# A hybrid decoder layer on one core: the down product written in a fixed order for three engines, its last block product bank by bank over five steps, and the row factors of the final norm in fewer operations

## The chip, the core and the metric

The kernel runs on one core of a Trainium2 chip. The metric is the device time of one execution in microseconds, the median over runs. One further execution was taken with the hardware profiler; its records are the trace that is read here.

## The reference

```python
def reference(x, mem, norm_mix, w_in, ..., w_up, conv_w, conv_b, w_down, norm_final):
    h = x
    for l in range(DEPTH):
        ...
        h = h + conv_ffn(rms_norm(h, norm_ffn[l]), w_up[l], conv_w[l], conv_b[l], w_down[l])
    return rms_norm(h, norm_final)

def conv_ffn(h, w_up, conv_w, conv_b, w_down):
    u = h @ w_up
    ...
    gate, val = jnp.split(u, 2, axis=-1)
    return (jax.nn.silu(gate) * val) @ w_down
```

What is left out is the token mixing, the cross attention and a causal convolution of width 3. All in fp32: 1024 rows of 1024, one layer, and an inner width of 2816. The change touches the last product, `(silu(gate) * val) @ w_down` (1024 x 2816 by 2816 x 1024), the residual sum with `h` and the final `rms_norm`.

## The kernel before

A fp32 product is made of three fp32r matmuls. `split` (L105) turns a source tile of 128 x 512 into an *operand*: ScalarE casts it to its high part (L109), VectorE subtracts that from the source to get the low part (L110), and TensorE adds up high x high, high x low and low x high. An operand pair (left and right) is used in one *step*: four PSUM banks (128 rows of the output by 512 columns each) times three matmuls, 12 in all (L1331).

`ffn_down` computes the down product in a Winograd form: the 1024 x 2816 left factor and the 2816 x 1024 right one are cut into 2 x 2 blocks, a11 to a22 and b11 to b22, and seven block products of 11 steps each, P1 to P7, are made of the blocks and of sums and differences of them. The sums and differences are tile operations of VectorE, made by `comb` (L1317). In order: P1 = a11 b11 into the banks x (named psT, psO, psF, psS); P2 = a12 b21 into the banks y; P3 = s1 b11, with s1 = a21 + a22 and then a11 replaced by s1 - a11, into new banks y after P2's are copied away by ScalarE (L1451); P4 = a11 t2, onto x, with t2 = b22 - b11 and b21 replaced by b21 - t2; P5 = s3 (b22 - b12), with s3 = a22 - a11, onto x; P6 = a22 b21, onto x; P7 = s4 b22, with s4 = a12 - a11, onto P3's y. Between products, quarters of the output come out of the banks: a *snapshot* (L1366) adds a bank to a tile of residual rows, while the bank goes on to be added to by the next product; a *half row* (L1371) does so for the last time and has ScalarE sum the squares of the result (L188); a *gain* (L1376) multiplies by the final norm's weight. When both halves of four rows' squares are there, `row_factors` makes 1/sqrt(mean + eps) of them (an Ln and an Exp on ScalarE, L175 and L176, and a Newton step of four small VectorE operations, L179 to L182), and `finish` multiplies the halves by it, one on ScalarE (L1391), one on VectorE (L1394), and sends them out, the one through SyncE's queue, the other through ScalarE's.

What sets the order around the change:

- Operands sit in six slots, three pairs, so the casts of pair k wait until TensorE has ended step k - 3.
- `product` takes a list `before` (run ahead of the first step), a list `later` (spread over the steps) and calls `more`, which makes the operand pair two steps ahead (`AHEAD` = 2); it calls for the sources (`left(k)`, `right(k)`, that is the combinations) one step further ahead than the pair itself.
- A scheduler decides in which order each engine gets the instructions of the down phase, by priorities and by its own estimate of when they become ready. TensorE, VectorE and ScalarE each run their instructions in the order so fixed.
- P7 is written with `tail=3`: its steps 0 to 7 go through the four banks in turn, and then each bank gets its last three steps together, so that bank 0 is done first.
- Blocks of the left factor come back from DRAM (`g_d`) by SyncE's queue into three stage buffers (`st`) of two steps each.

Of the kernel before, what the change touches and what calls it, by code (L numbers as in the profile page):

```python
# [19 lines left out]
F32R = mybir.dt.float32r  # L20
# [7 lines left out]
P = 128  # L28
# [32 lines left out]
class Layer:  # L61
# [1242 lines left out]
    def ffn_down(self, pre, hcnew):  # L1304
# [9 lines left out]
        acc = self.small("facc", [P, NT, 2], bufs=1)  # L1314

# [4 lines left out]
        def operand(src):  # L1320
            t = self.wslot("w", (P, 2, 512))
            self.split(src, t[:, 0], t[:, 1])
            return t

        def product(ps, left, right, first, before=(), later=(), ops=(), tail=1):


            def step(i, k, g, w):
# [5 lines left out]
            ops, later = list(ops), list(later)  # L1334
            srcs = [None] * len(ops)

            def more(k):
                while len(srcs) <= min(k + 1, n - 1):
                    srcs.append((left(len(srcs)), right(len(srcs))))
                if len(ops) <= k < n:  # L1340
                    ops.append(tuple(operand(t) for t in srcs[k]))
# [36 lines left out]
        def row_factors(t, count):  # L1378

            ssq, r = self.small("fssq", [P, 4])[:, :count], self.small("frs", [P, 4])[:, :count]  # L1380
            guess, newton = self.rsqrt_steps(r, ssq, D, count)

            def first():
                tt(out=ssq, in0=acc[:, t:t + count, 0], in1=acc[:, t:t + count, 1], op=add)
                guess()
            return r, [first, newton]

        def finish(t, r, done, dc, todo, tc):
# [91 lines left out]
        def s4(k):  # L1480
            if k % 2 == 1:
                take(a12s, 1)
# [127 lines left out]
```

## Time and profile before

| | us |
|---|---|
| three runs | 1331.81, 1331.30, 1329.92 |
| median | 1331.30 |
| profiled execution | 1331.28 |
| its span in the trace | 1329.2 |
| down product, first to last matmul | 1106.18 to 1319.83 |
| output after the last matmul | 9.37 |

The span is the time from the first to the last record; 2.08 us of the execution lie outside it. A row of the timeline begins with its start and its length in us, names the engine, the line, the operation and out<-in, and ends with the idle time before it and what ended that. A row of a table of windows has the stretch, its length, each engine's busy time with the number of its instructions, the TensorE clock granted (1.00 is full), the DMA share and GB/s. In a row of the waits view stand the waiting engine, tile and line, what it waited for, the sum, the count and the longest wait.

### The profile page before, as it was taken

What the parts mean: (1) busy time and instruction counts of PE and PEld (TensorE: products, weight loads), DVE (VectorE), ACT (ScalarE), POOL (GpSimd) and SP (SyncE); (2) the same over time, 40 slices, a digit from 0 to 9 for tenths busy, and PEclk for the clock granted to TensorE, in tenths of its full rate; (3) what the DMA queues carried; (4) which work ended last, traced back from release to release, by engine and by line L of the source; (5) the groups of instructions that cost most, each with busy time, mean ns of one, the idle gap of its engine ahead of it and who ended that gap; (6) DMA issues with size and microseconds to landing.
All of it is one profiled execution on the core that took longest, in us unless ns stands there. A gap on an engine that the chain in (4) does not pass through costs nothing.

```text
span 1329.2 us, 17255 instructions
## 1 busy us (share of the span) xinstructions
PE 1307.0 (98%) x6575; PEld 1083.6 (82%) x6575; DVE 918.0 (69%) x1564; ACT 587.6 (44%) x1041; POOL 86.6 (7%) x150
## 2 busy tenths in 40 slices
PE   8999999999999999999999999999999999999997
PEld 8887777988888888888888888888888888888785
DVE  6939763377544333564469998888888877998766
ACT  6525544345433233453344544444443444454454
POOL 1400111101100000001100000000000000000000
PEclk9999999999999999999999999999999999999999
DMA  7632112148744312143322343232223239710204
GB/s 219 187 110 64 61 56 60 64 149 278 201 155 138 127 48 64 32 153 94 87 64 64 111 134 114 85 96 73 75 91 96 69 109 328 255 64 8 72 18 149
DMA packets 141528, 146.89 MB, mean 111 GB/s; under 512 B 15825, under 2 KB 108166, under 8 KB 141446
## 3 DMA queue, kind: packets, MB, share of 16 engines
q1 hardware_dynamic: 129974, 111.02, 27.1%
q0 software_dynamic: 10304, 32.68, 7.0%
q10 hardware_dynamic: 1168, 2.10, 0.4%
q8 instruction: 51, 0.84, 0.2%
q14 instruction: 31, 0.25, 0.1%
HBM read 109.06 MB, written 38.28 MB: 111 GB/s over the span
## 4 chain that ended last, share of the span: by engine, by line
PE 50%; issue 37%; DVE 6%; DMA 3%; POOL 2%; ACT 1%; SPq 0%; POOLq 0%; DVEq 0%; ACTq 0%
PE psF L140 10%; PE psF L141 10%; PE psF L142 10%; PE psF L1331 4%; PE psS L1331 3%; DVE w L110 2%; PE psT L1331 1%; PE psO L1331 1%; PE psO L140 1%; PE psO L141 1%; PE psO L142 1%; PE psO L964 1%; PE psS L911 1%; PE psS L951 1%; POOL g_d L1264 1%
## 5 line engine op out<-in xcount | busy, mean ns | idle before, releaser
L109 ACT CAST w<-st 128x1024 fp32r<-128x1024 f32 (+1 forms) x162 | 142.5, 883 | 282.9 <-PE psF L141 110.0
L110 DVE TENSOR_TENSOR w<-st,w 128x1024 fp32r<-128x1024 f32 (+1 forms) x162 | 163.6, 1012 | 86.4 <-ACT w L109 85.8
L1253 DVE SCALAR_TENSOR_TENSOR uy<-uy,vec,uy 128x1023 f32<-128x1023 f32 (+1 forms) x88 | 112.1, 1280 | 1.1 <-ACT uy L1251 0.7
L1331 PE MATMUL psF<-w,w 128*128 128x512 f32 x330 | 92.9, 390 | 0.1
L1331 PE MATMUL psS<-w,w 128*128 128x512 f32 x330 | 92.4, 389 | 0.0
L1224 PE MATMUL psS<-a,w 128*128 128x512 f32 x360 | 86.5, 389 | 0.0
L140 PE MATMUL psF<-xh,w 128*128 128x512 f32 x208 | 83.3, 400 | 0.0
L142 PE MATMUL psF<-xh,w 128*128 128x512 f32 x208 | 81.5, 392 | 0.0
L141 PE MATMUL psF<-xl,w 128*128 128x512 f32 x208 | 81.1, 390 | 0.0
L1224 PEld LDWEIGHTS psS<-a,w 128*128 128x128 f32 x360 | 67.6, 188 | 14.0
L1224 PE MATMUL psF<-a,w 128*128 128x512 f32 x324 | 77.8, 389 | 0.0
L1331 PEld LDWEIGHTS psF<-w,w 128*128 128x128 f32 x330 | 61.7, 188 | 13.9 <-DVE w L110 0.8
L1331 PEld LDWEIGHTS psS<-w,w 128*128 128x128 f32 x330 | 61.9, 188 | 12.9
L1224 PEld LDWEIGHTS psF<-a,w 128*128 128x128 f32 x324 | 60.8, 188 | 12.6
L140 PE MATMUL psF<-act,w 128*128 128x512 f32 x176 | 69.4, 395 | 0.0
L141 PE MATMUL psF<-act,w 128*128 128x512 f32 x176 | 69.0, 392 | 0.0
L142 PE MATMUL psF<-act,w 128*128 128x512 f32 x176 | 68.7, 390 | 0.0
L1251 ACT ACTIVATE uy<-uy,vec 128x1024 f32<-128x1024 f32 x44 | 54.8, 1246 | 25.3 <-DVE uy L1244 17.2
L1224 PE MATMUL psS<-act,w 128*128 128x512 f32 x240 | 57.8, 389 | 0.0
L1224 PE MATMUL psS<-act,wx 128*128 128x512 f32 x240 | 57.6, 389 | 0.0
L1224 PEld LDWEIGHTS psS<-act,wx 128*128 128x128 f32 x240 | 45.1, 188 | 9.4
L1224 PEld LDWEIGHTS psS<-act,w 128*128 128x128 f32 x240 | 45.0, 188 | 9.4
(394 smaller groups left out, 3013.4 us busy)
## 6 DMA issues: line engine op xcount, KB each, us to landing
st<-in_w_up_dram SPq DMA_DIRECT2D x44, 512.0 KB, 4.0
g_d<-uy POOLq DMA_DIRECT2D x22, 512.0 KB, 2.9
act<-in_w_down_dram SPq DMA_DIRECT2D x12, 512.0 KB, 9.1
st<-g_d SPq DMA_DIRECT2D x10, 512.0 KB, 3.9
res<-g_d SPq DMA_DIRECT2D x10, 512.0 KB, 9.1
st<-in_w_in_dram SPq DMA_DIRECT2D x9, 512.0 KB, 6.7
xt_d<-pts POOLq DMA_DIRECT2D x16, 256.0 KB, 5.0
ow_d<-pts POOLq DMA_DIRECT2D x32, 128.0 KB, 3.2
```

The lines of the kernel that those rows point to most:

```text
L109: h = nc.scalar.copy(out=hi, in_=src)
L110: l = nc.vector.tensor_tensor(out=lo, in0=src, in1=hi.bitcast(F32), op=ALU.subtract)
L140: mm(out, lhsT=lh, rhs=rh, start=start, stop=False)
L141: mm(out, lhsT=lh, rhs=rl, start=False, stop=False)
L142: mm(out, lhsT=ll, rhs=rh, start=False, stop=stop)
L911: nc.tensor.matmul(ps[u][g][:, t, :nk], lhsT=self.sq[2 * u + t][pr, q], rhs=self.sk[pr, k0:k0 + nk], start=True, stop=True)
L951: nc.tensor.transpose(pp[:, 2 * u + t], probs[u][:, 2 * g + t, j * P:(j + 1) * P], self.ident)
L964: nc.tensor.matmul(po[64 * g:64 * g + 64], lhsT=self.sv[:, k0 // P + j, 64 * g:64 * g + 64], rhs=pts[2 * j + g], start=j == 0, stop=j == n ...
L1224: nc.tensor.matmul(ps, lhsT=b[l][:, q], rhs=a[q][r], start=first and q == 0 and n == 0, stop=first and q == 3 and n == 2, skip_group_check ...
L1251: nc.scalar.activation(out=y, in_=u, func=AF.Identity, scale=self.v("cw2", j), bias=self.v("conv_b", j))
L1253: nc.vector.scalar_tensor_tensor(out=y[:, s:], in0=u[:, :T - s], scalar=self.v(nm, j), in1=y[:, s:], op0=ALU.mult, op1=ALU.add)
L1331: nc.tensor.matmul(ps[i], lhsT=g[:, l, tk], rhs=w[:, r], start=first and k == 0 and m == 0, stop=first and k == n - 1 and m == 2, skip_gro ...
```

## The change

Four things change in `ffn_down`, and one in `run`:

1. The down phase runs under `manual_schedule` for TensorE, VectorE and ScalarE: these get their instructions in the order in which the code issues them. The code is arranged for it: `more` makes a pair's combinations directly ahead of its operands, with no step further ahead; both of the first pairs are made before the `before` list; `later` is spread evenly over the steps, or given by step.
2. P6's four half rows move from `before` to `later`, followed by the four gains and by six combinations of P7 (s4 of steps 0 to 5). The loads of a12 for these are issued ahead of P6.
3. P7 goes bank by bank over its last five steps (`tail=5`). The pairs of steps 8 to 10 go into slots of their own (`pre`, six), and `ahead` says after which step each pair is made: 2, 3, then 4 and 8, 5 and 9, 6, then 7 and 10. Its half rows of rows 4 to 7 stand after steps 0 and 1; the factors and outputs of these rows after step 5; behind each bank's last step stand its half row, its factor and its output (`done`).
4. `row_factors` keeps one part of the mean (`known`) beforehand and does the rest in fewer operations on the way: for a single row four of VectorE after the sum of squares, where there were six. The VectorE half of an output goes through GpSimd's queue, except the last row's.

```diff
-            def step(i, k, g, w):
+        def product(ps, left, right, first, before=(), later=(), ops=(), tail=1, ahead=None, done=()):
+
+
+
+
+            def step(i, k):
+                g, w = ops[k]
                 tk = slice(i * P, (i + 1) * P)
...
-
-            more(0)
+                if k < n and k not in ops:
+                    new = pre if ahead and k >= n - 3 else self.wnew
+                    ops[k] = tuple(operand(t, new) for t in (left(k), right(k)))
+
+            if not isinstance(later, dict):
+                later = {k: later[len(later) * k // steps:len(later) * (k + 1) // steps] for k in range(steps)}
+            for k in range(AHEAD):
+                more(k)
             for f in before:
                 f()
-            more(AHEAD - 1)
-            for k in range(n):
-                if k < n - tail:
-                    for i in range(4):
-                        step(i, k, *ops[k])
-                elif k == n - tail:
-                    for q in range(k, n):
-                        more(q)
-                    for i in range(4):
-                        for q in range(k, n):
-                            step(i, q, *ops[q])
-                more(k + AHEAD)
-                cut = len(later) // (n - k) if k < n - 1 else len(later)
-                for f in later[:cut]:
+            for k in range(steps):
+                for i in range(4):
+                    step(i, k)
+                for q in ahead[k] if ahead else [k + AHEAD]:
+                    more(q)
+                for f in later.get(k, ()):
                     f()
-                later = later[cut:]
+            for i in range(4):
+                for k in range(steps, n):
+                    step(i, k)
+                for f in done[i:i + 1]:
+                    f()
 
         def snapshot(ps, dst, t, c):
 
@@ -1375,24 +1376,39 @@
         def gain(dst, c):
             return lambda: tt(out=dst, in0=dst, in1=nfin[:, 512 * c:512 * c + 512], op=mult)
 
-        def row_factors(t, count):
-
-            ssq, r = self.small("fssq", [P, 4])[:, :count], self.small("frs", [P, 4])[:, :count]
...
+        def row_factors(t, count, c):
+
+
+            stt = nc.vector.scalar_tensor_tensor
+            m, v, y, z, r = (fac[:, x, t:t + count] for x in range(5))
+
+            def known():
+                nc.vector.tensor_scalar(out=m, in0=acc[:, t:t + count, 1 - c], scalar1=1.0 / D, scalar2=EPS, op0=mult,
+                                        op1=add)
+
+            def guess():
+                stt(out=v, in0=acc[:, t:t + count, c], scalar=1.0 / D, in1=m, op0=mult, op1=add)
+                nc.scalar.activation(out=z, in_=v, func=AF.Ln)
+                nc.scalar.activation(out=y, in_=z, func=AF.Exp, scale=-0.5)
+                nc.vector.tensor_scalar(out=v, in0=v, scalar1=-0.5, scalar2=None, op0=mult)
+
+            def newton():
+                if count == 1:
+                    stt(out=m, in0=y, scalar=y, in1=v, op0=mult, op1=mult)
+                else:
+                    tt(out=m, in0=y, in1=y, op=mult)
+                    tt(out=m, in0=m, in1=v, op=mult)
+                stt(out=r, in0=m, scalar=1.5, in1=y, op0=add, op1=mult)
+            return r, [known, guess, newton]
+
+        def finish(t, r, done, dc, todo, tc, queue=nc.gpsimd):
 
             def f():
                 nc.scalar.mul(out=done, in_=done, mul=r)
                 nc.sync.dma_start(out=self.out[0, t * P:(t + 1) * P, 512 * dc:512 * dc + 512], in_=done)
                 sl = slice(512 * tc, 512 * tc + 512)
                 nc.vector.scalar_tensor_tensor(out=todo, in0=todo, scalar=r, in1=nfin[:, sl], op0=mult, op1=mult)
-                nc.scalar.dma_start(out=self.out[0, t * P:(t + 1) * P, sl], in_=todo)
+                queue.dma_start(out=self.out[0, t * P:(t + 1) * P, sl], in_=todo)
             return f
 
         def take(gen, count):
@@ -1445,9 +1461,6 @@
             comb(a21[k], a21[k], a22[k], add)
             comb(a11[k], a21[k], a11[k], sub)
             return a21[k]
-        def c11_done(i, ps):
-            nc.scalar.copy(out=c12[i], in_=ps)
-            half_row(c12[i], c11[i], i, 0)()
         done = [lambda i=i, ps=y[i]: nc.scalar.copy(out=c12[i], in_=ps) for i in range(4)]
         late = [half_row(c12[i], c11[i], i, 0) for i in range(4)]
         y = [self.bank(r) for r in "FSFS"]
@@ -1467,40 +1480,37 @@
 
...
+            if k in (2, 8, 9):
                 take(a12s, 1)
-            return comb(a12[k], a12[k], a11[k], sub)
-        r, steps = row_factors(4, 4)
-        product(y, s4, lambda k: b22[k], False, [half_row(x[i], c21[i], 4 + i, 0) for i in range(4)],
-                steps + [finish(4 + i, r[:, i:i + 1], c22[i], 1, c21[i], 0) for i in range(4)], tail=3)
-        for i in range(2):
-            half_row(y[i], c12[i], i, 1)()
-        r, (first, newton) = row_factors(0, 2)
-        first()
-        half_row(y[2], c12[2], 2, 1)()
-        newton()
-        for i in range(2):
-            finish(i, r[:, i:i + 1], c11[i], 0, c12[i], 1)()
-        r, (first, newton) = row_factors(2, 1)
-        first()
-        half_row(y[3], c12[3], 3, 1)()
-        newton()
-        finish(2, r, c11[2], 0, c12[2], 1)()
-        r, steps = row_factors(3, 1)
...
+        halves = [half_row(x[i], c21[i], 4 + i, 0) for i in range(4)]
+        factors = [row_factors(i, 1, 1) for i in range(4)]
+        later = {0: halves[:2], 1: halves[2:], 5: [*steps, *(known for _, (known, _, _) in factors)] +
+                 [finish(4 + i, r[:, i:i + 1], c22[i], 1, c21[i], 0) for i in range(4)]}
+
+        def last(i):
...
 
 
 # ---- launch: one core; inputs and outputs as the reference has them ----

...

```

VectorE around the end of P4, before. `st` and `act` are the sources of P5 that L1317 makes (s3 and b22 - b12), `w` are operands, `c12` the rows that the snapshots L1366 fill from the four x banks; a row with x2 stands for two steps, and the rows ahead of `w<-st1650` belong to P4's last pairs:

```order
L110 TENSOR_TENSOR w1646_10179<-act01493_9233,w1646_10179 128x512
L110 TENSOR_TENSOR w1647_10182<-st1638_10129,w1647_10182 128x512
L1317 TENSOR_TENSOR st1653_10250<-res1550_9508,pre1487_9221 128x512 x2
L110 TENSOR_TENSOR w1648_10198<-act01495_9237,w1648_10198 128x512
L110 TENSOR_TENSOR w1649_10201<-st1645_10176,w1649_10201 128x512
L1317 TENSOR_TENSOR st1658_10291<-res1552_9512,pre1489_9225 128x512 x2
L110 TENSOR_TENSOR w1651_10240<-st1650_10235,w1651_10240 128x512
L110 TENSOR_TENSOR w1652_10243<-act11511_9291,w1652_10243 128x512
L110 TENSOR_TENSOR w1654_10253<-st1650_10235,w1654_10253 128x512
L1366 TENSOR_TENSOR c121525_9312<-psT1517_9304,c121525_9312 128x512
L1366 TENSOR_TENSOR c121526_9313<-psO1518_9305,c121526_9313 128x512
L1366 TENSOR_TENSOR c121527_9314<-psF1519_9306,c121527_9314 128x512
```

And now. L1318 is the combination, L1377 a gain, L1367 a snapshot:

```order
L1377 TENSOR_TENSOR c111524_9313<-c111524_9313,nfin1483_9215 128x512
L1377 TENSOR_TENSOR c111525_9314<-c111525_9314,nfin1483_9215 128x512
L1318 TENSOR_TENSOR st1651_10238<-res1549_9507,pre1486_9218 128x512
L1318 TENSOR_TENSOR act11512_9294<-res1588_9754,act11512_9294 128x512
L110 TENSOR_TENSOR w1652_10241<-st1651_10238,w1652_10241 128x512
L110 TENSOR_TENSOR w1653_10244<-act11512_9294,w1653_10244 128x512
L1318 TENSOR_TENSOR st1651_10238<-res1549_9507,pre1486_9218 128x512
L1318 TENSOR_TENSOR act11512_9294<-res1588_9754,act11512_9294 128x512
L110 TENSOR_TENSOR w1654_10249<-st1651_10238,w1654_10249 128x512
L110 TENSOR_TENSOR w1655_10252<-act11512_9294,w1655_10252 128x512
L1367 TENSOR_TENSOR c121526_9315<-psT1518_9307,c121526_9315 128x512
L1367 TENSOR_TENSOR c121527_9316<-psO1519_9308,c121527_9316 128x512
```

The combinations s3 of P5's steps 2 to 5 (`st1653`, `st1658`) stood among P4's last subtractions, those of steps 0 and 1 earlier still. Now those of steps 0 and 1 stand behind the gains, each step's directly ahead of its two subtractions, the snapshots follow the second pair, and the later combinations come behind the snapshots.

VectorE at the beginning of P7, before: the `w` are the pairs of steps 0 to 2, L1371 half rows of rows 4 to 7, the combination the one of step 6:

```order
L110 TENSOR_TENSOR w1714_10709<-res1587_9751,w1714_10709 128x512
L110 TENSOR_TENSOR w1719_10725<-st1704_10691,w1719_10725 128x512
L1371 TENSOR_TENSOR res1547_9502<-psT1517_9304,res1547_9502 128x512
L1371 TENSOR_TENSOR res1547_9502<-psO1518_9305,res1547_9502 128x512
L1371 TENSOR_TENSOR res1549_9506<-psF1519_9306,res1549_9506 128x512
L1371 TENSOR_TENSOR res1549_9506<-psS1520_9307,res1549_9506 128x512
L110 TENSOR_TENSOR w1720_10728<-res1587_9751,w1720_10728 128x512
L110 TENSOR_TENSOR w1722_10746<-st1705_10693,w1722_10746 128x512
L1317 TENSOR_TENSOR st1712_10703<-st1712_10703,act01491_9229 128x512
L110 TENSOR_TENSOR w1723_10749<-res1588_9753,w1723_10749 128x512
```

Now, a little later in P7, pairs 4 to 9 (`pre` are the operands of steps 8 to 10):

```order
L110 TENSOR_TENSOR w1721_10780<-st1681_10476,w1721_10780 128x512
L110 TENSOR_TENSOR w1722_10783<-res1590_9758,w1722_10783 128x512
L1318 TENSOR_TENSOR st1723_10786<-st1723_10786,act01494_9234 128x512
L110 TENSOR_TENSOR pre1724_10789<-st1723_10786,pre1724_10789 128x512
L110 TENSOR_TENSOR pre1725_10792<-res1592_9762,pre1725_10792 128x512
L110 TENSOR_TENSOR w1726_10807<-st1681_10476,w1726_10807 128x512
L110 TENSOR_TENSOR w1727_10810<-res1590_9758,w1727_10810 128x512
L1318 TENSOR_TENSOR st1723_10786<-st1723_10786,act01494_9234 128x512
L110 TENSOR_TENSOR pre1729_10816<-st1723_10786,pre1729_10816 128x512
L110 TENSOR_TENSOR pre1730_10819<-res1592_9762,pre1730_10819 128x512
L1318 TENSOR_TENSOR st1712_10730<-st1712_10730,act01492_9230 128x512
```

Five of P7's combinations stood well ahead of their subtractions; now those of steps 8, 9, 6, 7 and 10 stand directly ahead of theirs, and subtractions for steps 8 and 9 stand among those of 4 and 5.

VectorE at the end, before: half rows of rows 0 to 2 from the y banks with the small operations of the factors between them:

```order
L1371 TENSOR_TENSOR c121525_9312<-psF1592_9761,c121525_9312 128x512
L1371 TENSOR_TENSOR c121526_9313<-psS1593_9762,c121526_9313 128x512
L1384 TENSOR_TENSOR fssq1743_10959<-facc1484_9216 128x2
L174 TENSOR_SCALAR rs_v1745_10961<-fssq1743_10959 128x2
L1371 TENSOR_TENSOR c121527_9314<-psF1594_9763,c121527_9314 128x512
L179 TENSOR_TENSOR rs_t1746_10962<-rs_y1747_10963 128x2
L180 TENSOR_TENSOR rs_t1746_10962<-rs_t1746_10962,rs_v1745_10961 128x2
L181 TENSOR_SCALAR rs_t1746_10962<-rs_t1746_10962 128x2
```

Now, from the outputs of rows 4 to 7 on, through bank 0 to the half row of bank 1:

```order
L1410 SCALAR_TENSOR_TENSOR res1548_9505<-res1548_9505,ffac1485_9217,nfin1483_9215 128x512 x2
L1410 SCALAR_TENSOR_TENSOR res1550_9509<-res1550_9509,ffac1485_9217,nfin1483_9215 128x512 x2
L1372 TENSOR_TENSOR c121526_9315<-psF1593_9764,c121526_9315 128x512
L1390 SCALAR_TENSOR_TENSOR ffac1485_9217<-facc1484_9216,ffac1485_9217 128x1
L1393 TENSOR_SCALAR ffac1485_9217<-ffac1485_9217 128x1
L1397 SCALAR_TENSOR_TENSOR ffac1485_9217<-ffac1485_9217 128x1
L1401 SCALAR_TENSOR_TENSOR ffac1485_9217<-ffac1485_9217 128x1
L1410 SCALAR_TENSOR_TENSOR c121526_9315<-c121526_9315,ffac1485_9217,nfin1483_9215 128x512
L1372 TENSOR_TENSOR c121527_9316<-psS1594_9765,c121527_9316 128x512
```

The outputs of rows 4 to 7 stood within P7's subtractions and now stand behind all of them and ahead of bank 0's half row; a bank's half row, its factor and its product are together, one bank after another.

More of the change, by code (lines that the diff above doesn't have):

```diff
@@ L1314, in ffn_down @@
         acc = self.small("facc", [P, NT, 2], bufs=1)
+        fac = self.small("ffac", [P, 5, NT], bufs=1)
         def comb(out, x, y, op):
@@ L1318, in comb, with operand @@
             return out
-        def operand(src):
-            t = self.wslot("w", (P, 2, 512))
+        def operand(src, new=self.wnew):
+            t = new(*(("w", (P, 2, 512), F32R, NW) if new is self.wnew else ("pre", (P, 2, 512), F32R, 6)))
             self.split(src, t[:, 0], t[:, 1])
             return t
-        def product(ps, left, right, first, before=(), later=(), ops=(), tail=1):
-            def step(i, k, g, w):
+        def product(ps, left, right, first, before=(), later=(), ops=(), tail=1, ahead=None, done=()):
+            def step(i, k):
+                g, w = ops[k]
                 tk = slice(i * P, (i + 1) * P)
```

41 lines of the change are left out of this document (20 added, 21 removed).

## The prediction

> **What bounds the kernel now.** I read the page first: busy times and the chain that ended last.
>
> ```profile
> PE 1307.0 (98%) x6575; PEld 1083.6 (82%) x6575; DVE 918.0 (69%) x1564; ACT 587.6 (44%) x1041; POOL 86.6 (7%) x150
> PE 50%; issue 37%; DVE 6%; DMA 3%; POOL 2%; ACT 1%; SPq 0%; POOLq 0%; DVEq 0%; ACTq 0%
> ```
>
> TensorE is busy for 98% of the span, so the change can only win what TensorE still waits for, and the tail behind it; it can lose without limit if TensorE is made to wait. The change touches the down projection alone. So I cut the span at its seven block products, P1 to P7, and the tail.
>
> ```profile
> core 0: us, PE busy (x) PEld busy (x) DVE busy (x) ACT busy (x) POOL busy (x), PEclk, DMA share, GB/s
> 1106.18:1137.56 31.38, 30.79 (x133) 24.54 (x132) 27.31 (x41) 14.93 (x23) 0.53 (x1) 1.00 0.91 328
> 1137.56:1167.48 29.92, 29.92 (x133) 24.75 (x132) 29.92 (x51) 13.92 (x25) 0.00 (x0) 1.00 0.53 183
> 1167.48:1197.86 30.38, 30.26 (x133) 24.67 (x132) 29.43 (x49) 15.56 (x32) 0.00 (x0) 1.00 0.21 70
> 1197.86:1227.78 29.92, 29.92 (x133) 24.77 (x132) 24.34 (x40) 12.57 (x22) 0.00 (x0) 1.00 0.03 9
> 1227.78:1258.20 30.42, 30.08 (x133) 24.59 (x131) 22.48 (x38) 12.87 (x23) 0.00 (x0) 1.00 0.24 78
> 1258.20:1289.60 31.40, 30.50 (x133) 24.95 (x134) 21.86 (x36) 15.52 (x32) 0.00 (x0) 1.00 0.01 2
> 1289.60:1319.83 30.23, 30.23 (x133) 24.29 (x131) 22.90 (x46) 18.00 (x40) 0.00 (x0) 1.00 0.32 113
> 1319.83:1329.20 9.37, 0.00 (x1) 0.00 (x0) 4.25 (x17) 3.48 (x10) 0.00 (x0) 0.71 0.61 224
> ```
>
> P2 and P4 run unbroken: 29.92 us, that is 11 steps of 2.72, or 132 matmuls 0.227 apart. Seven such products and the 0.16 that the last matmul's row outlasts its slot make 209.6; from 1106.18 to 1319.83 are 213.65. **TensorE loses 4.0 us in this whole phase**, 3.9 before P7 starts at 1289.60 (183.42 less 6 x 29.92) — all there is to win there. VectorE is full in P2 and P3 (29.92 of 29.92, 29.43 of 30.38): whatever is put there later must find room elsewhere. The waits between engines in this phase:
>
> ```profile
> ACT w L109 <- PE psS L1331: 95.0, 61, 2.3
> DVE w L110 <- ACT w L109: 24.2, 21, 1.4
> PEld psT L1331 <- DVE w L110: 3.1, 4, 1.2
> ```
>
> So casts wait for TensorE to free an operand slot (three pairs, so pair k waits for the end of step k-3), each subtraction waits for its cast, and TensorE hardly waits at all. Its stalls, and what delayed VectorE at the first:
>
> ```profile
> 1115.19 0.73 PE L1331 MATMUL psT<-w,w 128*128 128x512 f32 x2 [0.47 <-DVE w L110]
> 1258.32 0.93 PE L1331 MATMUL psT<-w,w 128*128 128x512 f32 x3 [0.45 <-DVE act L1366]
> 1263.01 0.73 PE L1331 MATMUL psT<-w,w 128*128 128x512 f32 x2 [0.78 <-DVE w L110]
> ```
>
> ```profile
> 1112.10 0.69 DVE L1317 TENSOR_TENSOR pre<-act,pre 128x512 f32<-128x512 f32 x1 [0.55 <-DMA act<-in_w_down_dram]
> 1112.71 1.22 DVE L1263 TENSOR_TENSOR uy<-uy,uy 128x1024 f32<-128x1024 f32 x1
> ```
>
> A combination of P2 stood ahead of a subtraction that P1 needed, and waited for a load. At the start of P6 eight bank operations in a row did the same.
>
> **Unit costs.** VectorE and ScalarE, back to back:
>
> ```profile
> 1257.48 0.69 DVE L1366 TENSOR_TENSOR act<-psT,act 128x512 f32<-128x512 f32 x1
> ...
> 1261.67 0.68 DVE L1371 TENSOR_TENSOR act<-psS,act 128x512 f32<-128x512 f32 x1
> 1262.27 0.68 DVE L110 TENSOR_TENSOR w<-act,w 128x512 fp32r<-128x512 f32 x1
> ```
>
> ```profile
> 1284.21 0.62 ACT L109 CAST w<-st 128x512 fp32r<-128x512 f32 x1 [1.58 <-PE psS L1331]
> 1284.74 0.61 ACT L109 CAST w<-res 128x512 fp32r<-128x512 f32 x1
> 1166.04 0.58 ACT L1451 COPY c<-psF 128x512 f32<-128x512 f32 x1
> ```
>
> ```profile
> 1284.87 0.69 DVE L110 TENSOR_TENSOR w<-st,w 128x512 fp32r<-128x512 f32 x1 [1.42 <-ACT w L109]
> 1318.44 0.15 DVE L179 TENSOR_TENSOR rs_t<-rs_y 128x2 f32<-128x2 f32 x1
> 1318.62 0.16 DVE L180 TENSOR_TENSOR rs_t<-rs_t,rs_v 128x2 f32<-128x2 f32 x1
> ```
>
> Eight operations from 1257.48 to 1262.27: 0.60 us from start to start, though each lasts 0.69. An operation that needs the one before starts only 0.03 after its end (1318.44 + 0.15 to 1318.62), so a dependent pair costs 0.73. A cast takes 0.62, 0.53 start to start, and the subtraction starts 0.04 after it (1284.83 to 1284.87). A cast that waits for a combination therefore puts 0.69 + 0.04 + 0.62 + 0.04 = 1.39 between that combination's start and the subtraction's.
>
> **What the change takes away.** In written order each pair's combinations stand directly ahead of its subtractions and none a step further ahead. P1's stalls go, as do those at P6's start, where four half rows move into later steps: gain 3.9, all before P7 (bounds 1.7, the idle of the three rows above, and 3.9).
>
> **What it adds at P3's start: 0.7 us.** The copies that free P2's banks stand behind the casts of P3's second pair; these now wait for a combination that stands behind P2's last subtractions and three snapshots. From the end of P2's eighth step: 0.69 to the subtraction, 5 x 0.60 to the first combination, 0.73 to its cast, 0.65 to the subtraction, 2 x 0.60 to the next combination, 0.73 to its cast, 2 x 0.53 to the copy, 0.63 for the copy: 8.69. TensorE is there after three steps less 0.16, 8.0. Bounds 0 (before, the copy at 1166.04 was in time) and 1.
>
> **What it adds at P5's start: 3.6 us.** P5 writes onto the banks that P4 filled last, after a snapshot of each. Before, VectorE made P5's combinations a step ahead and ran the snapshots early. Now these stand behind everything else of P4: per pair two combinations, the second needing the first, and two subtractions (0.73 + 3 x 0.60 = 2.5, with up to 0.1 of waiting for a cast: about 2.6), and eight half rows and gains at 0.60 spread over the steps. That is 3.2 us per step against TensorE's 2.72. Count from P4's first matmul: pair 3's slot is free at 2.72 + 0.16, its cast begins at 2.92, its subtractions at 3.57 and 4.17, the next operation at 4.77. From there stand eight half rows and gains (4.8), seven pairs (18.1), P5's first two pairs (2 x 2.58 = 5.2) and one snapshot (0.69): it ends at 33.5. TensorE is ready at 29.92: **3.6 idle**. By pitch alone (44 operations x 0.60 + 0.69) it would be 2.0; with every operation at its full 0.69, 5.9 at 44 x 0.69 + 0.69. I take 3.6, as the rows of dependent pairs stand nearest. P6's start then holds: in P5 a step has only four operations. On SyncE's queue three loads of P7's blocks now stand ahead of those of four residual tiles; each lands in about 4 us (row below) and P6 lasts 29.92, so neither is late.
>
> **The clock behind that gap: 1.7 us.**
>
> ```profile
> 313.40:316.80 3.40, 1.55 (x13) 1.55 (x14) 3.40 (x5) 1.89 (x4) 1.20 (x3) 1.00 0.54 143
> 316.82:320.23 3.41, 3.41 (x18) 3.41 (x18) 3.27 (x15) 1.72 (x8) 1.54 (x3) 0.50 0.87 303
> 340.70:344.12 3.42, 0.99 (x7) 0.79 (x7) 1.82 (x4) 3.42 (x8) 0.00 (x0) 1.00 0.00 0
> 344.12:347.54 3.42, 3.42 (x17) 3.36 (x16) 2.34 (x3) 0.59 (x1) 1.39 (x2) 0.50 0.81 251
> ```
>
> Twice a stretch of 3.4 us with TensorE busy under half of it was followed by 3.41 us at granted clock 0.50, which costs half of 3.41. An idle of 3.6 leaves some such stretch nearly empty, wherever they are cut; one window follows: 1.7 (bounds 0 and 3.4, two windows). The Trainium skill, "TensorE: Matmul & The Clock Gate", section "Why this matters for your kernels", warns of idle gaps over about 3 us and lowers the clock after one window of idle. Read as a window wholly idle, that rule would nearly always spare a gap of 3.6; the rows here, 1.55 and 0.99 busy in windows that were followed by half clock, speak against that reading.
>
> **What it adds in P7: 5.0 us.** Times from P7's first matmul, in the written order. ScalarE, in order, has the sums of squares of two half rows ahead of each of the casts of pairs 3 and 4, so those come late: subtractions of pair 2 at 0.85 and 1.45, half rows 2.05 and 2.65, sums from 2.78 and 3.55 (0.63 and 0.19 each), cast 3 at 4.19, its subtractions 4.84 and 5.44, half rows 6.04 and 6.64, sums 6.77 and 7.54, cast 4 at 8.18, subtractions 8.83 and 9.43. Then five pairs, each with its combination directly ahead: 1.39 + 0.60 + 0.60 = 2.6. Pair 8 from 10.03, pair 5 (1.2, no combination), 9, 6, 7, and 10, whose last subtraction starts at 23.5 and ends at 24.2. Pair 8's load waits for the buffer that pair 3's subtractions leave at 6.0, and lands just in time:
>
> ```profile
> st<-g_d SPq DMA_DIRECT2D x10, 512.0 KB, 3.9
> ```
>
> TensorE needs pair 10 at six steps (16.32) and four steps of one bank (4 x 0.68), 19.2: **5.0 late**. Before, these combinations had been made earlier, and P7 took 30.23. Bounds: 0, by 27 operations at 0.60, and 5.0 with all waits, nearest to which stands the chain of 1.39. TensorE then ends 24.26 + 0.62 + 3 x 3.40 = 35.1 after P7's start.
>
> **The tail.** Before:
>
> ```profile
> 1320.62 0.69 DVE L1371 TENSOR_TENSOR c<-psS,c 128x512 f32<-128x512 f32 x1
> 1322.63 0.20 ACT L175 ACTIVATE rs_t<-rs_v 128x1 f32<-128x1 f32 x1 [0.32 <-DVE rs_v L174]
> 1324.41 0.75 DVE L1394 SCALAR_TENSOR_TENSOR c<-c,frs,nfin 128x512 f32<-128x512 f32 x1
> ```
>
> From the end of the matmuls at 1319.83 (the window row) to the end of the last product with the row factor (1325.16) passed 5.33, and the outputs took another 4.04, to 1329.20. Now VectorE comes out of pair 10 at 24.2 with the factors of rows 4 to 7 (about 1.6: eight dependent small operations and two on ScalarE at 0.15 to 0.20) and four products with them (0.75 long, 0.67 apart: 2.7) still ahead of the first bank: half row 0 starts at 28.5, bank 0 having been ready at 24.9. Each bank is then one chain: half row 0.69, sum of squares 0.73 with its hidden read, four small operations at 0.16 and 0.20 on the way to the estimate and two behind it, the product 0.67 to the next half row, gaps 0.03 to 0.04: about 3.24, against 3.40 of TensorE per bank. The backlog stays: half row 3 at 28.5 + 9.7 = 38.2, although its bank is ready at 35.1, and the last product ends at 38.2 + 3.24 + 0.08 = 41.5. The row factors' fewer operations are in that 3.24. The last output leaves on ScalarE's queue as before: 4.04 more, 45.5 after P7's start against 1329.20 - 1289.60 = 39.6. **P7 and tail together: +5.9.** A lowered clock in P7's own gaps would delay banks that VectorE isn't ready for, and cost nothing. The output DMAs moved to GpSimd's queue are those of earlier rows, off the end.
>
> **The sum.** Against the profiled execution's span: -3.9 + 0.7 + 3.6 + 1.7 + 5.9 = +8.0, from 1329.2 to 1337.2; with the 2.08 us outside the span (1331.28 - 1329.2) 1339.3. That execution is the median of 1331.3 within 0.02. I say **1339**.
>
> **Rivals.**
> - *Faster: VectorE keeps the pace.* If P4's chain ends by 29.9, P5 starts on time and its clock stays full, and if P7's pairs meet 19.2 as well, TensorE ends at 30.1 and the last chain starts there: P7 and tail 30.1 + 3.3 + 4.0 = 37.4, or -2.2. -3.9 + 0.7 - 2.2 gives 1325.9. It decides at whether P4's 44 operations and the snapshot, from 4.77 to 29.9, can go at 0.55 each; the eight in the row above took 0.60. 0.08.
> - *No measurable change: the handovers overlap.* P5's stall at its lower bound of 2.0 and without a lowered clock, and in P7 the casts run ahead far enough that only half of the 5.0 is left: then the tail's backlog falls by 2.5 as well. -3.9 + 0.7 + 2.0 + 3.4 = +2.2: 1333.5. For it: bounds by pitch. Against it: the subtraction at 1284.87 did wait for its cast, and the order has nothing else to run there. 0.12, half of it within 0.2%.
> - *The clock stays full* behind P5's gap, because no whole stretch of 3.4 falls into it: 1337.6. 0.2. This is what the Trainium skill's clock gate page, named above, gives if its window must be idle throughout.
> - *P5's stall nearer 5, or two windows at half clock*: 1339.3 + 1.7 = 1341. 0.1.
> - *The change doesn't change the order:* the order of the new program has the rows moved, so it does; no chance given.
>
> **How the numbers follow.** The forecast has 0.5. Faster is the first rival with a little of the second; same, half of the second and a part of neighbouring cases; 0.2% (1328.6 to 1334.0) is about what a measurement of this kernel tells from no change. The range, 1333 to 1342, leaves out the first rival and the far ends.
>
> **What would show it.** A stall of 2 to 5 us ahead of P5's first matmul, released by a snapshot of VectorE, and a window at granted clock near 0.5 behind it. No stall at 1115 and at P6's start. In P7 TensorE's fifth and later steps waiting for subtractions, with ScalarE's sums of squares ahead of the casts of pairs 3 and 4. VectorE busy without a gap from pair 10 to the end, and half row 3 starting some 3 us after the last matmul. Were P4's VectorE seen idle between its operations, the sum would be wrong there.

## The result, and the profile after

| | us |
|---|---|
| before, median | 1331.3 |
| after, median of 5 runs (1351.67 to 1354.43) | 1351.9 |
| ratio, 95% interval | 1.0162 [1.0148, 1.0176] |
| forecast | 1339, range 1333 to 1342 |
| span of the profiled execution, before and after | 1329.2, 1349.8 |

The change made the kernel slower, as forecast, but by 20.6 us instead of 8. The windows of the changed kernel, cut at the same places: first the 11.31 us by which the down product starts later, with the up projection's matmuls (L1224) in them, then P1, P2, P3, P4 with the gap behind it, P5, P6, P7 and the tail.

```profile
core 0: us, PE busy (x) PEld busy (x) DVE busy (x) ACT busy (x) POOL busy (x), PEclk, DMA share, GB/s
1106.18:1117.49 11.31, 11.31 (x50) 9.15 (x49) 5.17 (x8) 3.91 (x6) 0.00 (x0) 1.00 0.95 348
1117.49:1147.43 29.94, 29.94 (x133) 24.78 (x132) 19.13 (x26) 14.92 (x23) 0.53 (x1) 1.00 0.90 324
1147.43:1178.24 30.81, 30.09 (x134) 24.60 (x132) 25.56 (x41) 13.10 (x24) 0.00 (x0) 1.00 0.55 200
1178.24:1208.29 30.05, 30.05 (x133) 24.89 (x133) 28.56 (x46) 14.07 (x25) 0.00 (x0) 1.00 0.08 27
1208.29:1242.38 34.09, 30.08 (x133) 24.61 (x132) 33.35 (x54) 15.20 (x30) 0.00 (x0) 1.00 0.11 39
1242.38:1274.01 31.63, 31.62 (x132) 25.86 (x132) 27.23 (x45) 12.86 (x22) 0.00 (x0) 0.95 0.22 75
1274.01:1304.26 30.25, 30.18 (x133) 24.89 (x133) 24.07 (x40) 15.03 (x30) 0.00 (x0) 1.00 0.01 2
1304.26:1341.60 37.34, 34.33 (x133) 26.28 (x131) 25.87 (x57) 20.65 (x46) 3.26 (x6) 0.91 0.33 118
1341.60:1349.80 8.20, 0.00 (x0) 0.00 (x0) 3.04 (x9) 2.57 (x6) 0.54 (x1) 0.70 0.36 135
```

From the down product's start to the end of the span there are 232.3 us (1349.8 - 1117.49) against 223.0 before (1329.2 - 1106.18): +9.3, where the forecast had +8.0. The other **11.3 us lie ahead of the down product**, in code that the diff doesn't touch. They are in no gap: TensorE is busy in all of that window. The groups of TensorE's instructions, by line and shape, before and then after (a group's busy time, then the mean ns of one):

```profile
L1224 PE MATMUL psS<-a,w 128*128 128x512 f32 x360 | 86.5, 389 | 0.0
L1224 PE MATMUL psS<-act,wx 128*128 128x512 f32 x240 | 57.6, 389 | 0.0
L140 PE MATMUL psS<-act,w 128*128 128x512 f32 x48 | 18.7, 389 | 0.0
```

```profile
L1224 PE MATMUL psS<-a,w 128*128 128x512 f32 x360 | 87.2, 391 | 0.0
L1224 PE MATMUL psS<-act,wx 128*128 128x512 f32 x240 | 59.3, 396 | 0.0
L140 PE MATMUL psS<-act,w 128*128 128x512 f32 x48 | 19.0, 396 | 0.0
```

Behind the arrow stand the moving operand (`rhs` in the program) and then the weights (`lhsT`). In these groups a matmul whose moving operand is an `act` tile takes 7 ns longer, in the other groups of L140 to L142 with `act` 5 to 6. All groups with `act` and `a` together are busy 11.3 us longer than before: 6.1 in L1224 with `act`, 1.4 with `a`, and 3.8 in L140 to L142. Other groups differ by up to 1.5 us, in both directions.

The stalls and the tail behave as forecast. TensorE's rows at the starts of P3 and P5 and in P7, and VectorE's at the end:

```profile
1178.24 0.96 PE L1335 MATMUL psF<-w,w 128*128 128x512 f32 x3 [0.72 <-ACT c L1464]
1242.38 1.49 PE L1335 MATMUL psT<-w,w 128*128 128x512 f32 x3 [4.01 <-DVE c L1367]
1322.61 0.51 PE L1335 MATMUL psF<-w,w 128*128 128x512 f32 x1 [1.56 <-ACT w L109]
1325.27 2.03 PE L1335 MATMUL psF<-w,w 128*128 128x512 f32 x3 [1.12 <-ACT w L109]
1339.37 2.21 PE L1335 MATMUL psS<-pre,pre 128*128 128x512 f32 x9
```

```profile
1332.76 0.68 DVE L1372 TENSOR_TENSOR c<-psF,c 128x512 f32<-128x512 f32 x1
1342.59 0.68 DVE L1372 TENSOR_TENSOR c<-psS,c 128x512 f32<-128x512 f32 x1
1345.19 0.75 DVE L1410 SCALAR_TENSOR_TENSOR c<-c,ffac,nfin 128x512 f32<-128x512 f32 x1
```

P3 waits 0.72 and P5 4.01; the three matmuls behind that gap take 1.49 instead of 0.84, at a lowered clock (P5's window is 31.63 long instead of 29.92). The first stretch of P5:

```profile
1242.38:1245.78 3.40, 3.40 (x8) 2.69 (x9) 3.24 (x6) 1.04 (x2) 0.00 (x0) 0.52 0.27 82
```

P7 starts at 1304.26: half row 0 follows 28.5 behind that, half row 3 38.3, and the last product ends 41.7 behind it.

### The profile page after: what moved, and what is told of

Read it like the earlier page. It is cut to its first block, busy times and chain, and to the rows that moved or that the text cites. A ratio compares the mean times of both kernels' runs of the same rounds, so it can differ in the third digit from the quotient of the medians.

```text
span 1349.8 us, 17277 instructions
## 1 busy us (share of the span) xinstructions
PE 1321.8 (98%) x6575; PEld 1087.4 (81%) x6575; DVE 923.8 (68%) x1566; ACT 590.5 (44%) x1043; POOL 90.3 (7%) x157
## 4 chain that ended last, share of the span: by engine, by line
PE 90%; DVE 4%; ACT 2%; issue 2%; DMA 1%; POOL 0%; SPq 0%; DVEq 0%; ACTq 0%; POOLq 0%
PE psS L1224 14%; PE psF L1224 13%; PE psF L140 12%; PE psF L141 12%; PE psF L142 12%; PE psF L1335 4%; PE psS L1335 4%; PE psT L1335 2%; PE psO L1335 2%; PE psS L140 1%; PE psS L142 1%; PE psS L141 1%; PE psO L140 1%; PE psO L141 1%; PE psO L142 1%
## 5 line engine op out<-in xcount | busy, mean ns | idle before, releaser
L1335 PE MATMUL psF<-w,w 128*128 128x512 f32 x312 | 89.9, 396 | 3.7 <-ACT w L109 2.7
L1335 PE MATMUL psS<-w,w 128*128 128x512 f32 x312 | 87.5, 390 | 0.0
L1224 PE MATMUL psS<-a,w 128*128 128x512 f32 x360 | 87.2, 391 | 0.0
L140 PE MATMUL psF<-xh,w 128*128 128x512 f32 x208 | 83.1, 400 | 0.0
L142 PE MATMUL psF<-xh,w 128*128 128x512 f32 x208 | 81.5, 392 | 0.0
L1224 PEld LDWEIGHTS psS<-a,w 128*128 128x128 f32 x360 | 67.6, 188 | 15.1
L1224 PE MATMUL psF<-a,w 128*128 128x512 f32 x324 | 78.5, 391 | 0.0
L1335 PEld LDWEIGHTS psF<-w,w 128*128 128x128 f32 x312 | 59.0, 190 | 18.2 <-ACT w L109 3.5
L1224 PEld LDWEIGHTS psF<-a,w 128*128 128x128 f32 x324 | 60.9, 188 | 13.6
L140 PE MATMUL psF<-act,w 128*128 128x512 f32 x176 | 70.3, 400 | 0.0
L141 PE MATMUL psF<-act,w 128*128 128x512 f32 x176 | 70.0, 398 | 0.0
L142 PE MATMUL psF<-act,w 128*128 128x512 f32 x176 | 69.7, 396 | 0.0
L1335 PEld LDWEIGHTS psS<-w,w 128*128 128x128 f32 x312 | 58.9, 189 | 12.4
L1224 PE MATMUL psS<-act,w 128*128 128x512 f32 x240 | 59.4, 396 | 0.0
L1224 PE MATMUL psS<-act,wx 128*128 128x512 f32 x240 | 59.3, 396 | 0.0
L1224 PEld LDWEIGHTS psS<-act,w 128*128 128x128 f32 x240 | 45.1, 188 | 10.8
L1224 PEld LDWEIGHTS psS<-act,wx 128*128 128x128 f32 x240 | 45.1, 188 | 10.7
```

The lines of the kernel that those rows point to most:

```text
L140: mm(out, lhsT=lh, rhs=rh, start=start, stop=False)
L141: mm(out, lhsT=lh, rhs=rl, start=False, stop=False)
L142: mm(out, lhsT=ll, rhs=rh, start=False, stop=stop)
L1224: nc.tensor.matmul(ps, lhsT=b[l][:, q], rhs=a[q][r], start=first and q == 0 and n == 0, stop=first and q == 3 and n == 2, skip_group_check ...
L1335: nc.tensor.matmul(ps[i], lhsT=g[:, l, tk], rhs=w[:, r], start=first and k == 0 and m == 0, stop=first and k == n - 1 and m == 2, skip_gro ...
```

## Experiments

Two questions: what slowed matmuls that nobody touched, and whether the rest is the order's, as the forecast has it.

### Where the tiles lie

The changed kernel has other small tiles (one new, two gone), together 32 bytes a partition less, so the pools that are stacked above them moved down by 32 bytes; those stacked from the upper end of SBUF stayed. The first `act` tile starts at byte 12256 before and 12224 after; the first operand slot `w` stays at 204768, `wx` at 118752, `a` at 143328. In bytes beyond a multiple of 512, `w`, `wx`, `a` and `act` all lay at 480 before; now `act` lies at 448. The `a` rows became 2 ns slower although neither `a` nor its `w` moved; the runs do not show why. I moved tiles in both kernels.

`b_addr0`, the kernel before with `act` where the change puts it:

```diff
-ssq, r = self.small("fssq", [P, 4])[:, :count], ...
+ssq, r = self.small("fssq", [P, 4], bufs=2)[:, :count], ...
```

> The kernel before, with one small factor tile given two buffers instead of three, so that all that lies above it in SBUF moves down by 32 bytes; no engine's order changes. The tiles of activations ('act'), which are the moving operand of 1584 matmuls, then start at a multiple of 64 bytes, as they do in the changed kernel, instead of 32 beyond one. Theory A (the address is what made the matmuls on act take 396 instead of 389 ns, ahead of the down product and outside the written order): about +11 us, 1342, with act rows at 396 ns. Theory B (the written order itself reached back into the phases ahead of it): no change, 1331, rows at 389 ns.

Measured: 1340.76, ratio to before 1.0073 [1.0057, 1.0090]. From its groups:

```profile
L1224 PE MATMUL psS<-act,wx 128*128 128x512 f32 x240 | 59.3, 396 | 0.0
```

`a_addr32`, the changed kernel with `act` back at 12256:

```diff
 self.tiny = e(tc.tile_pool(name="tiny", bufs=3))
+self.tiny.tile([P, 8], F32, name="pad", tag="pad", bufs=1)
```

> The changed kernel with 32 unused bytes in the pool of small tiles, so that act lies where it lay before (32 beyond a multiple of 64). Theory A: the down product starts at about 1106 instead of 1117.5 and the time is 1340 to 1341, close to what the sum of the prediction gave; what is left against before (about +9) is the order's. Theory B: 1352, unchanged.

Measured: 1339.52, ratio 1.0063 [1.0048, 1.0078]; the down product starts at 1105.15, and the rows with `act` are back at 389 (L1224 is L1225 in this run):

```profile
L1225 PE MATMUL psS<-act,wx 128*128 128x512 f32 x240 | 57.7, 389 | 0.0
```

Address and order are thus told apart from both sides: 32 bytes cost the kernel before 0.73%, and without them the change costs 0.63%. The two don't quite make up the whole: 9.7 and 8.4 us are 18.1 of 20.6, and taken out of the changed kernel the 32 bytes are worth 12.4. What the remaining 2.5 us are is open.

`b_both32` moves the upper pools too, apart from the operand slots:

```diff
+ssq, r = self.small("fssq", [P, 4], bufs=2)[:, :count], ...
 self.wnew = wstack.enter_context(self.pool("wpool", "right"))
+self.wnew("pad", (P, 8))
```

> The kernel before with the lower pools 32 bytes down and the upper pools 32 bytes down too, the operand slots w excepted, to see which address counts. Moving operand act and loaded weights wx both at a multiple of 64; act and a at a multiple of 64 with w 32 beyond one; w with w, both 32 beyond. Theory A1 (the moving operand alone counts): act with wx 396 ns, a with w 396, x with w 396, w with w 389, in all some 3300 matmuls at +7 ns, about 1354. Theory A2 (it is the difference of the two operands' addresses that costs): act with wx back at 389, a, x, act with w at 396, about 1351.

Measured: 1345.44 (one run). Its groups:

```profile
L1224 PE MATMUL psS<-a,w 128*128 128x512 f32 x360 | 88.8, 395 | 0.0
L1224 PE MATMUL psS<-act,wx 128*128 128x512 f32 x240 | 57.9, 390 | 0.0
L141 PE MATMUL psF<-x,w 128*128 128x512 f32 x128 | 50.7, 396 | 0.0
```

`act` and `wx`, both 32 bytes down, are fast again; `a` and `x`, which lay well before, are now slow, because `w` hasn't moved with them. The moving operand's own address is not what counts: theory A2 holds in these rows. A2's 1351 was too high all the same: some `w` tiles of the up projection had moved along, the penalty is nearer 6 ns than 7 in these groups, and the 192 matmuls of 256 columns with the moving tile `wg` became 2.4 us faster, which neither theory had.

`b_addr64`, the kernel before with the lower pools 64 bytes down:

```diff
-ssq, r = self.small("fssq", [P, 4])[:, :count], ...
+ssq, r = self.small("fssq", [P, 4], bufs=1)[:, :count], ...
```

> The kernel before with the lower pools 64 bytes down (one buffer of the small tile instead of three): act again 32 beyond a multiple of 64, but at another residue of 128 than w. If the residue of 64 is what counts: act rows at 389 ns, 1331. If that of 128: 396 ns, 1342.

Measured: 1340.93 (one run), and

```profile
L1224 PE MATMUL psS<-act,wx 128*128 128x512 f32 x240 | 59.2, 394 | 0.0
```

Lying alike within 64 bytes isn't enough: the period within which the two must lie alike is at least 128 bytes. Whether it is 128, 256 or 512 the runs do not tell.

### The order

`a_sched` gives the three engines back to the scheduler, over the changed code.

```diff
-with self.tc.manual_schedule(engines={mybir.EngineType.PE, mybir.EngineType.DVE,
-                                     mybir.EngineType.Activation}):
-    list(down)
+list(down)
```

> The changed kernel with act at its old address (as a_addr32) and without the fixed order: the scheduler orders the three engines again, over the same code (P7 bank by bank over five steps, halves and combinations moved to P6, the shorter row factors). Theory C (the order is what costs: VectorE's queue at P5 and in P7): the stall of 4.0 at P5, the half clock behind it and P7's 5.0 go, and the tail keeps the shorter factors: 1326 to 1330, faster than before. Theory D (what costs is the arrangement itself, P7's five late pairs with their combinations and the outputs of rows 4 to 7 behind them): still 1335 or more.

Measured: 1330.97, ratio 1.0001 [0.9992, 1.0009]. The costs go with the order, as C says, but the gain that I expected on top does not come:

```profile
1132.65 0.74 PE L1335 MATMUL psT<-w,w 128*128 128x512 f32 x2 [0.69 <-DVE w L110]
1172.39 0.96 PE L1335 MATMUL psS<-w,w 128*128 128x512 f32 x3 [1.96 <-ACT c L1464]
```

```profile
1321.79 0.69 DVE L1372 TENSOR_TENSOR c<-psS,c 128x512 f32<-128x512 f32 x1
1324.40 0.75 DVE L1410 SCALAR_TENSOR_TENSOR c<-c,ffac,nfin 128x512 f32<-128x512 f32 x1
```

The tail got shorter: from the last half row to the end of the last product 3.36 us, against 4.54 before (1320.62 to 1325.16). The scheduler gave that back with stalls of its own, 1.96 at a copy in P3 among them: from the first matmul of the down product to the last it took 215.0 us, 1.4 more than before, and from there to the end of the span 7.6, 1.8 less. So the remaining parts of the change, together, are worth nothing under the scheduler.

`a_gains_p6` takes the four gains out of P4:

```diff
-product(x, lambda k: a11[k], t2, False, later=late+[gain(c11[i], 0) for i in range(4)])
+product(x, lambda k: a11[k], t2, False, later=late)
 ...
-later = [half_row(y[i], c22[i], 4 + i, 1) for i in range(4)] + [gain(c22[i], 1) for i in range(4)]
+later = [half_row(y[i], c22[i], 4 + i, 1) for i in range(4)] + [gain(c11[i], 0) for i in range(4)]
+later += [gain(c22[i], 1) for i in range(4)]
```

> a_addr32 with one thing changed: the four gains that the written order puts into P4 are put into P6. Theory C: VectorE's chain ahead of P5's snapshot gets 4 x 0.60 = 2.4 us shorter, the stall at P5 falls from 4.0 to about 1.6, and the clock is not lowered behind it (another 1.4): 1339.5 - 3.8 = 1335.7. Rival (the snapshot waits for P4's banks or for operand slots, not for VectorE's queue): stall 4.0, 1339.5.

Measured: 1335.77, ratio 1.0039 [1.0025, 1.0052]. The stall, and the two stretches behind it:

```profile
1226.49 0.93 PE L1335 MATMUL psT<-w,w 128*128 128x512 f32 x3 [1.50 <-DVE c L1367]
```

```profile
1226.50:1229.90 3.40, 3.40 (x15) 2.81 (x16) 3.24 (x6) 1.05 (x2) 0.00 (x0) 1.00 0.26 82
1229.90:1233.30 3.40, 3.40 (x17) 2.81 (x16) 3.24 (x6) 1.30 (x3) 0.00 (x0) 1.00 0.21 77
```

VectorE's queue in P4 is the cause of P5's stall, and without the long gap the clock stays at 1.00.

`a_p7_order` changes P7's order alone (C[k] makes the combination of step k, T loads two more blocks of a12, H are the half rows; in `product` an entry that can be called is called in its place):

```diff
-ahead=[[2], [3], [4, 8], [5, 9], [6], [7, 10]]
+ahead=[[T, 2, H[0], H[1]], [C[6], C[7], 3, H[2]], [T, 4, H[3], C[8]], [C[9], 5, 8], [T, 6, 9], [C[10], 7, 10]]
```

> a_addr32 with P7's order alone changed: its half rows spread over four steps, the combinations of steps 6 to 10 a pair or more ahead of their casts, the loads of a12 a little earlier; P5 and the tail's order stay. Theory C (five pairs, each with combination, cast and subtraction in a row, hold VectorE up in P7): TensorE's waits in P7 fall from 3.0 or more to about 0.8, pair 10 is ready some 4 us earlier, and the end comes about 5 us earlier: 1334.5. Rival (VectorE has too much to do in P7 whatever the order): no more than 1 us, 1338.5 or above.

Measured: 1334.78, ratio 1.0031 [1.0019, 1.0043]. In P7 one wait of TensorE is left, where `a_addr32` has three (1.59, 0.31 and 1.11):

```profile
1311.37 0.73 PE L1335 MATMUL psF<-w,w 128*128 128x512 f32 x2 [0.71 <-DVE w L110]
```

The same operations fit; they stood in a bad order.

`a_tail_mixed` changes the tail's order alone. `finish` returns its two halves apart, and in each bank's chain stand:

```diff
 half_row(y[i], c12[i], i, 1)()
+outs[i][0]()
 ...
-finish(i, r, c11[i], 0, c12[i], 1, nc.scalar if i == 3 else nc.gpsimd)()
+g, h = finish(i, r, c11[i], 0, c12[i], 1, nc.scalar if i == 3 else nc.gpsimd)
+h()
+g()
+outs[i][1]()
```

> a_addr32 with one thing changed: the four products of rows 4 to 7 on VectorE no longer stand ahead of bank 0's half row; each stands behind one of the four half rows, where VectorE waits for ScalarE's sum of squares. Theory C (from pair 10 to the end VectorE's queue sets the time, not TensorE): TensorE ends as in a_addr32, half row 0 starts 2.7 us earlier, and the end comes about 2.6 us earlier: 1336.9. Rival (the last bank's end on TensorE sets the time): no change, 1339.5.

Measured: 1338.57, ratio 1.0054 [1.0041, 1.0068], 1 us instead of 2.6; as the interval overlaps that of `a_addr32`, even this gain isn't shown. Half row 0, and the last output issued:

```profile
1319.71 0.69 DVE L1372 TENSOR_TENSOR c<-psF,c 128x512 f32<-128x512 f32 x1 [0.98 <-PE psF L1335]
1334.59 0.33 SPq L1408 DMA_DIRECT2D out_dram<-act  x1
```

VectorE now comes too early and waits for bank 0: TensorE was itself late there, at a clock that was lowered behind its gaps in P7. A stretch ahead of bank 0's end:

```profile
1313.30:1316.70 3.40, 2.89 (x6) 2.01 (x7) 2.71 (x5) 1.58 (x3) 0.00 (x0) 0.50 0.00 0
```

I had counted that as free, which it is only as long as VectorE is later still. And the last output is now one of ScalarE's products for rows 4 to 7, 1.2 us behind VectorE's last. Neither engine alone set the end: in the changed kernel the half rows start only 1.6 us (bank 0) and 1.0 us (bank 3) after TensorE has ended their bank.

`a_rewritten` puts all of these together and moves the copies and snapshots ahead of a product's second pair:

```diff
-for k in range(AHEAD):
-    more(k)
+more(0)
 for f in before:
     f()
+more(AHEAD - 1)
```

> a_addr32 with a mended written order: the gains in P6, snapshots and copies ahead of a product's second pair, the products of rows 4 to 7 behind the last half rows, and in P7 the combinations of steps 6 to 10 a pair or more ahead of their casts, with the half rows spread over four steps. Theory C: P3's 0.7 goes, P5's stall falls to about 1.2 and P7's from 5.0 to about 1, and the tail follows TensorE again: 10 us less than 1339.5, 1328 to 1331, level with before or a little below. Theory D': a written order for these engines cannot keep up, as some wait of a cast always stands ahead of other work: 1334 or more.

Measured: 1329.17, ratio 0.9985 [0.9976, 0.9994], as theory C has it. At P3's start TensorE doesn't wait, at P5's 0.95, in P7 0.86. Its last product and last output:

```profile
1320.58 0.75 DVE L1412 SCALAR_TENSOR_TENSOR c<-c,ffac,nfin 128x512 f32<-128x512 f32 x1
1322.54 0.33 SPq L1408 DMA_DIRECT2D out_dram<-act  x1
```

`a_rewritten2` takes that last output out of the last chain:

```diff
-    outs[i][1]()
+    if i < 3:
+        outs[i + 1][1]()
 ...
+later[5].append(outs[0][1])
```

> a_rewritten with ScalarE's four products of rows 4 to 7 one chain earlier each, so that the last bank's chain has only its own. In a_rewritten the last output issued was one of them, 1.2 us behind the last of VectorE's. Theory: the span ends 1.2 us earlier, 1328.0, against before 0.2% faster. Rival (the outputs then queue behind each other anyway): 1329.2.

Measured: 1327.76, ratio 0.9982 [0.9973, 0.9991], the best of all: faster than before by 0.18%, just under what I had called measurable, with an interval clear of 1. Its step over `a_rewritten` isn't shown, as the two ratios' intervals overlap.

`a_rewritten3` adds 32 bytes to one more pool, so that `wg` lies at 480 too:

```diff
 with self.pool("p2") as new, self.tc.manual_schedule(engines={mybir.EngineType.PE}):
+    new("pad", (P, 8))
```

> a_rewritten2 with 32 unused bytes in one more pool, so that the tile wg, too, lies 32 beyond a multiple of 64 as its partner w does: 288 matmuls of wg with w and 96 with xh and xl change from unlike to like addresses. Theory A2: the rows of wg with w fall by some 3 to 7 ns a matmul, about 1 us in all, 1327. Rival A1 (the moving operand alone, slower at a multiple of 64): the rows with wg as the weights (w with wg) stay as they are, those with wg moving fall, half of it.

Measured: 1328.73, ratio 0.9987 [0.9978, 0.9995]: no gain in the time. The rows moved as A2 says, here with `wg` as the weights, in `a_rewritten2` and then in `a_rewritten3`:

```profile
L142 PE MATMUL psO<-w,wg 128*128 128x512 f32 x32 | 12.6, 394 | 0.0
```

```profile
L142 PE MATMUL psO<-w,wg 128*128 128x512 f32 x32 | 12.5, 390 | 0.0
```

That is the same moving tile at the same address, faster with its weights moved. TensorE's wait for VectorE ahead of the matmuls with `wg` as the moving operand grew from 2.0 to 2.9 meanwhile, which may be where the gain went; that wasn't tried.

## Why the prediction was right or wrong

The direction was right and the time lay outside the range. **The step that failed stands in its first part: "The change touches the down projection alone."** The sum took the 1106 us ahead of it as given. The order of the instructions there is unchanged; their addresses are not. With the address undone the changed kernel takes 1339.5 against the forecast 1339, and the address alone, put into the kernel before, costs 9.7 (1340.76 - 1331.1, the median of before beside it).

That 1339.5 meets 1339 so closely is partly luck. From the down product's start to the end of the span the change lost 9.3 us and not 8.0, and in the profiled execution of `a_addr32` the down product began 1.0 us earlier than before (1105.15 against 1106.18), for which the sum has no term; single executions of the kernels with `act` at its old address differ by up to 2.6 there. The 1.3 us by which the sum was short lie in P1 to P6: 186.77 against 183.42, +3.35 where the forecast's terms make +2.1.

By the prediction's steps:

- *P1's stalls go, gain 3.9.* P1 runs unbroken (29.94). P6 still loses 0.33 (30.25 against 29.92).
- *P3's start, 0.7.* 0.72 idle; P2's window is 0.89 longer than 29.92.
- *P5's start, 3.6.* 4.01 idle, P4's window 4.17 longer than 29.92, with VectorE's queue in P4 as the cause (`a_gains_p6`: 1.50 after 2.4 us of work were taken out).
- *The clock, 1.7.* P5's window is 1.71 longer than 29.92. A gap of 4.0 lowered it and one of 1.5 did not. The rival in which it stays full has fallen. (An idle of 3.6 need not leave a stretch "nearly empty, wherever they are cut": cut in the middle, each of two stretches is busy for 1.6.)
- *P7 5.0, and P7 with the tail +5.9.* From P7's start to the end of the span 45.54 (1349.8 - 1304.26) against 45.5 forecast. The chains were right too: half rows at 28.5 and 38.3 against 28.5 and 38.2, pair 4's first subtraction at 8.82 against 8.83, pair 10's last at 23.66 against 23.5. (Six steps and four of one bank make 19.04, not 19.2; the 5.0 barely moves.) TensorE's own end was 37.3 behind P7's start and not 35.1: the lowered clock in P7, which the end hides here, and `a_tail_mixed` brought out. So half row 3 starts 1.0 us after the last matmul, not "some 3".
- *Faster, VectorE keeps the pace:* fallen for the order as changed; the mended order nearly does (`a_rewritten2`: 1.00 idle at P5's start, 0.88 in P7).

The case of no measurable change, with half of P7's stall left, didn't come either: VectorE waited 0.69 to 0.76 us for the cast behind each of the five combinations in P7, until the order was changed. The first of them:

```profile
1314.29 0.68 DVE L1318 TENSOR_TENSOR st<-st,act 128x512 f32<-128x512 f32 x1
1315.66 0.69 DVE L110 TENSOR_TENSOR pre<-st,pre 128x512 fp32r<-128x512 f32 x1 [0.69 <-ACT pre L109]
```

## What to carry to other kernels

A new or removed tile, however small, can move all that is allocated above it, and here 32 bytes (9.7 us) cost more than the worst mistake in the order (P5's stall with the clock behind it, or P7 with the tail, 5.9 each). Before a change is judged by its time, compare the mean durations of untouched groups in both traces: 389 against 396 ns in a group that nobody edited says that part of the loss is not where the diff is. A hand-written order has to keep the work that makes an operand's source at least one operand ahead of the cast that reads it, for in the written order VectorE stood idle while it waited for that cast (0.69 in the row above); written so, it did 0.18% better than the scheduler's order in the kernel before.

## What the runs showed of the hardware

- In L1224 a matmul of 512 fp32r columns takes 389 to 391 ns in these records when its moving operand and its weights start at the same place in a period of at least 128 bytes, and 394 to 396 ns when they start 32 or 64 bytes apart. Both can be moved together without loss (`b_both32`: 390). Why, the runs do not show; nor were other widths or types tried on purpose. The rows of 256 columns with `wg` as the moving operand don't follow: 290 ns at 64 bytes apart in `b_both32`, 311 at 64 apart in the changed kernel, 294 alike in `a_rewritten3`.
- TensorE's clock was lowered behind a gap of 4.0 us and not behind one of 1.5, and also behind the gaps of 1.56, 0.3 and 1.12 us in P7, none of which lasts 3.4. Three stretches of the changed kernel's P7:

```profile
1321.40:1324.80 3.40, 1.24 (x3) 0.48 (x3) 1.97 (x4) 1.86 (x4) 0.00 (x0) 0.95 0.00 0
1324.80:1328.20 3.40, 2.92 (x6) 2.04 (x7) 2.71 (x5) 1.55 (x3) 0.00 (x0) 0.50 0.00 0
1328.20:1331.60 3.40, 3.40 (x10) 2.65 (x10) 2.96 (x14) 2.03 (x5) 0.34 (x1) 0.55 0.01 4
```

  The Trainium skill, "TensorE: Matmul & The Clock Gate", section "Why this matters for your kernels", speaks of idle gaps over about 3 us; by these rows several shorter ones together, with TensorE busy 1.24 of 3.40 us, are enough.
